# A written issue order for the attention of an encoder layer, and the zeros of its result rows moved into it

## The chip, the cores and the metric

One core of a Trainium2 chip runs the whole program. The metric is device time in microseconds: 1177.47 us is the median of three runs before the change (1177.21 to 1180.05). One more execution was taken with the hardware profiler; all rows here are of it.

## The reference

One layer of a streaming encoder for 1024 tokens of width 1024, in float32:

```
proj = x @ w_in                       -> q, k, v, u (512 columns each)
a    = differential attention          4 heads, each with two 64-wide score maps; a token sees
                                       its own chunk of 64 and all chunks before it:
       p0, p1 = softmax(q_c k_c / 8);  o = (p0 - lam * p1) @ v
       o = o * rsqrt(mean(o^2) + 1e-5) * subln_g * (1 - lam_init)
s    = S5 state space model on u, gelu, then z = z * sigmoid(z @ w_glu + b_glu)
h    = LayerNorm(alpha * x + concat([a, s]) @ w_out)
y    = LayerNorm(alpha * h + MoE(h))   32 experts in 4 groups, two experts per token
```

## The kernel before

The kernel is one straight program for five engines: TensorE (PE), ScalarE (ACT), VectorE (DVE), GpSimd (POOL) and SyncE (SP), which issues most of the transfers. A planner puts each engine's instructions into an order by a simulated time line; an instruction that is traced earlier has priority, but one that is ready sooner may pass it. Where `tc.add_manual_dep(i, earlier, NoSync)` is given, `i` is issued behind `earlier` on that engine, with no wait for its end. In the kernel before only the experts are ordered in this way, by `keep_order` at the end. SBUF is handed out in 25 buffers of 8 KB per partition, taken from a queue (`sl.get`) and given back (`sl.put`); a buffer's next user waits for its last.

In order of time: the projections of u, the state space model in eight units (`ssm_pair`, each followed by a projection of q or v as a filling), the projections of k, the attention, the mixing products with w_out and the first LayerNorm and routing, the experts, the last LayerNorm.

In the state space part `zeros(u)` writes zeros over `moe_dram`, the 2048 rows of results of the experts (8 MB), from one zeroed tile, two transfers of 1 MB behind each of the units 0 to 3. SP issues them, between the transfers of the state space model (`Tm`, line 581) and the loads of w_in (line 190).

The attention is cut into 32 units, a head h and a block i of 128 query rows; n = 128 (i + 1) keys are seen. Units 0 to 15 alternate head 0 with falling i and head 1 with rising i (sizes 1024, 128, 896, 256 and so on); units 16 to 31 take heads 2 and 3 with falling i, 1024 first. For one unit:

- `scores` (lines 792 and 793): two products for each map c and each 512 keys, the query as a high and a low part. For n up to 512 both maps lie in one PSUM pair; above, each map has a pair of its own. VectorE masks 64 rows with a memset (801 or 809) and takes the negative maximum (802 or 810). ScalarE makes the exponential and its row sum (795). Of the PSUM pairs there are two.
- `weigh`: VectorE makes 1/L (817), the factor rho and p0 + rho * p1 (both in the helper at 163); TensorE transposes the blocks (826); ScalarE copies the first four blocks and VectorE the others (827); TensorE adds up the output products (830).
- `normalize` once per four blocks of a head: copy and square on ScalarE (836, 838), a row sum and small products on VectorE (840, and the helpers at 157 and 169), a power on GpSimd (845), one more small product on VectorE, the scaling on GpSimd; `finish`, three units later, transposes and copies with the factor gcol (852, 853).

The loop traces for each u: the scores of unit u + 2 whole, then `weigh` of unit u, then a `finish`, then the fillings at fixed units: `ask` (queries of heads 2 and 3, units 6 and 12), `glu_prepare` (load of w_glu and splits, units 15 and 20), `glu` (12 products of 512 columns each, units 16 to 19 and 21 to 24), `wo_part` (load and split of a quarter of w_out, units 22, 24, 26 and 30). The splits of the fillings lie on ScalarE and GpSimd. In `glu` the gate is made by ScalarE (749) and GpSimd (169), and multiplied into zT by VectorE (helper at 157).

## Time and profile before

| | us |
|---|---|
| median of three runs | 1177.47 |
| the profiled execution, its own time | 1178.13 |
| its span, first to last instruction | 1176.4 |
| TensorE busy in it | 1083.7 (92%) |
| VectorE busy | 970.0 (82%) |
| ScalarE busy | 708.5 (60%) |
| GpSimd busy | 358.0 (30%) |

A row of a timeline has the start and the duration in us, engine, line, operation, written tile and read tiles; in brackets the idle time of the engine before it and what ended that. A line can be that of a small helper (154 subtract, 157 multiply, 160 add, 163 and 169 scalar forms, 173 the high part of a split), so the names of the tiles tell the step. A row of the groups by line has the count, then the busy time in us and the mean duration of one in ns, then idle time ahead. The starts and durations of TensorE's matmuls overlap, since they are pipelined; the step from one start to the next is what one costs.

### The profile page before, as it was taken

To read this page: it belongs to the slowest core of one execution; us is meant where nothing else is said; L and a number is where in the kernel's file an instruction comes from. 1 tells how busy PE (TensorE), PEld (TensorE's weight loads), DVE (VectorE), ACT (ScalarE), POOL (GpSimd) and SP (SyncE) were. 2 spreads that over 40 slices of the span, in tenths; PEclk is the share of its full clock that TensorE was granted. 3 is DMA by queue.
4 is the path that set the end of the run, shared out by engine and by line. 5 is a ranking of instruction groups with operands and counts; after the bars stand their busy time and mean duration, and the time that the engine had idled before them with its cause. 6 is when DMAs were issued, how large, how long until landed. Compare 5 with 4: busy or idle time off the path is not lost.

```text
span 1176.4 us, 15227 instructions
## 1 busy us (share of the span) xinstructions
PE 1083.7 (92%) x5345; PEld 903.9 (77%) x5345; DVE 970.0 (82%) x1434; ACT 708.5 (60%) x956; POOL 358.0 (30%) x296
## 2 busy tenths in 40 slices
PE   6979998897869989995999999999999999999994
PEld 5867887676758878885888888888888888888862
DVE  4898567556878785456899999999999999999976
ACT  3312332426756653212788888888888888888852
POOL 1077464312453454243121221221221211211133
PEclk9989999898999999996999999999999999999997
DMA  8537321201120346446599999999999999999593
GB/s 209 138 97 259 113 59 29 59 19 41 40 64 4 130 160 217 168 171 242 195 343 386 374 380 389 382 393 392 367 393 381 362 384 379 387 392 386 191 261 149
DMA packets 90686, 278.90 MB, mean 237 GB/s; under 512 B 29468, under 2 KB 49964, under 8 KB 66160
## 3 DMA queue, kind: packets, MB, share of 16 engines
q1 hardware_dynamic: 78080, 252.78, 57.6%
q0 software_dynamic: 11520, 24.83, 7.8%
q8 instruction: 43, 0.70, 0.2%
q10 hardware_dynamic: 1008, 0.30, 0.1%
q14 instruction: 35, 0.29, 0.1%
HBM read 254.12 MB, written 34.60 MB: 245 GB/s over the span
## 4 chain that ended last, share of the span: by engine, by line
PE 69%; DVE 12%; DMA 7%; ACT 4%; SPq 3%; issue 3%; POOL 1%; ACTq 0%; DVEq 0%; POOLq 0%
PE g L1251 15%; PE y L1242 15%; PE u L1251 14%; PE mix L1082 7%; PE proj L243 4%; DMA misc<-in_w_in_dram 3%; PE xT L1212 3%; DMA moe_dram<-zero 2%; PE glu L745 2%; PE po L830 2%; DVE ssm L157 1%; SPq L581 1%; PE hT L1224 1%; PE s L792 1%; PE pl L1104 1%
## 5 line engine op out<-in xcount | busy, mean ns | idle before, releaser
L1151 POOL DMA_INDIRECT moe_dram<-yo,idx x30 | 52.1, 1738 | 425.9 <-DVE yo L163 425.9
L243 PE MATMUL proj<-xh,wa 128*128 128x512 f32 x256 | 77.9, 412 | 4.4 <-ACT ssm L678 4.2
L243 PE MATMUL proj<-xh,wb 128*128 128x512 f32 x256 | 74.5, 404 | 1.6 <-ACT ssm L678 1.6
L1082 PE MATMUL mix<-woh,mx 128*128 128x512 f32 x256 | 73.8, 399 | 1.6 <-DVE mx L154 1.6
L1146 POOL DMA_INDIRECT gx<-h_dram,idx x32 | 60.4, 1889 | 22.5 <-DVE WT L160 13.1
L795 ACT ACTIVATE p<-s,nm 128x1024 f32<-128x1024 f32 (+7 forms) x64 | 47.2, 743 | 24.3 <-DVE nm L810 14.9
L243 PEld LDWEIGHTS proj<-xh,wa 128*128 128x128 f32 x256 | 50.2, 199 | 14.9 <-ACT ssm L678 4.5
L243 PEld LDWEIGHTS proj<-xh,wb 128*128 128x128 f32 x256 | 48.6, 194 | 11.5 <-ACT ssm L678 1.8
L1082 PEld LDWEIGHTS mix<-woh,mx 128*128 128x128 f32 x256 | 47.4, 189 | 11.2 <-DVE mx L154 2.1
L792 PE MATMUL s<-kk,qh 128*128 128x512 f32 (+3 forms) x96 | 37.6, 396 | 18.1 <-ACT p L795 15.0
L1258 ACT ACTIVATE yo<-y,WT 128x1024 f32<-128x1024 f32 (+1 forms) x33 | 36.0, 1091 | 24.4 <-PE y L1242 24.4
L1212 PEld LDWEIGHTS xT<-ident,gx 128*128 128x128 f32 x256 | 36.2, 208 | 9.7 <-DMA gx<-h_dram,idx 5.7
L243 PE MATMUL proj<-xl,wa 128*128 128x512 f32 x128 | 43.6, 412 | 0.0
L1212 PE MATMUL xT<-ident,gx 128*128 128x128 f32 x256 | 36.9, 287 | 6.9 <-DMA gx<-h_dram,idx 5.4
L163 DVE SCALAR_TENSOR_TENSOR yo<-gx,first,yo 128x1024 f32<-128x1024 f32 (+1 forms) x33 | 41.3, 1252 | 1.6
L154 DVE TENSOR_TENSOR xe<-xT,xe 128x1024 fp32r<-128x1024 f32 (+1 forms) x33 | 39.1, 1184 | 4.1 <-ACT xe L173 4.1
L830 PE MATMUL po<-vv,half 128*128 128x128 f32 x288 | 41.0, 285 | 1.4 <-ACT half L827 1.3
L1082 PE MATMUL mix<-wol,mx 128*128 128x512 f32 x128 | 42.1, 397 | 0.0
L243 PE MATMUL proj<-xl,wb 128*128 128x512 f32 x128 | 41.0, 397 | 0.0
L173 ACT CAST xe<-xT 128x1024 fp32r<-128x1024 f32 (+1 forms) x33 | 32.3, 978 | 13.4 <-PE xT L1212 13.4
L830 PEld LDWEIGHTS po<-vv,half 128*128 128x128 f32 x288 | 37.4, 198 | 3.5 <-ACT half L827 2.4
L792 PEld LDWEIGHTS s<-kk,qh 128*128 128x128 f32 x96 | 19.3, 201 | 24.7 <-ACT p L795 22.6
(864 smaller groups left out, 3560.1 us busy)
## 6 DMA issues: line engine op xcount, KB each, us to landing
misc<-in_w_in_dram SPq DMA_DIRECT2D x16, 512.0 KB, 3.9
moe_dram<-zero SPq DMA_DIRECT2D x8, 1024.0 KB, 8.5
xr<-in_x_dram SPq DMA_DIRECT2D x8, 512.0 KB, 8.8
wo_raw<-in_w_out_dram SPq DMA_DIRECT2D x4, 1024.0 KB, 5.1
xa<-in_x_dram SPq DMA_DIRECT2D x8, 512.0 KB, 4.4
h_dram<-xa SPq DMA_DIRECT2D x8, 512.0 KB, 3.6
mo<-moe_dram SPq DMA_DIRECT2D x8, 512.0 KB, 8.6
mo<-moe_dram POOLq DMA_DIRECT2D x8, 512.0 KB, 12.7
```

Of the source, the lines that this page charges most:

```text
L154: eng.tensor_tensor(out=out_, in0=a, in1=b, op=ALU.subtract)
L163: return V.scalar_tensor_tensor(out=out_, in0=a, scalar=s, in1=b, op0=op0, op1=op1)
L243: PE.matmul(o[:, hs], wt[kt // 4][:, w_, kt % 4, :], x_[:, hs], start=(kt == 0 and n == 0), stop=(kt == KT - 1 and n == 2))
L792: PE.matmul(s_[:, c0:c0 + w], qd[0][:, c, tk], kk[h][:, c, c0:c0 + w], start=True, stop=False)
L795: S.activation(p_[:, c, 0:n], s_[:, 0:n], AF.Exp, bias=nm[:, c:c + 1], accum_out=L[:, j, c:c + 1])
L830: PE.matmul(po[:, j * P:(j + 1) * P], aT[:, k, :], vv[k // 4][:, k % 4, h * P:(h + 1) * P], start=(k == 0), stop=(k == i))
L1082: PE.matmul(o[-(hs.start > 0)][:, hs], mx[:, m_, kt, :], (woh, wol)[w_][kt // 2][:, kt % 2, hs], start=(kt == 0 and n == 0), stop=(kt == K ...
L1146: return G.indirect_dma_start(out=dst, out_offset=None, in_=h_dram[:, :], in_offset=bass.IndirectOffsetOnAxis(ap=ix, axis=0), bounds_check ...
L1151: G.indirect_dma_start(out=moe_dram[:, :], out_offset=bass.IndirectOffsetOnAxis(ap=ix, axis=0), in_=src, in_offset=None, bounds_check=2 * ...
L1212: PE.transpose(b_[:, kt * P:(kt + 1) * P], rows(g_, kt), ident)
L1242: PE.matmul(y[h_], hid[e][:, x_, kt, :], w_[:, k, HALVES[h_]], start=(kt == 0 and n == 0), stop=(kt == 3 and n == 2))
L1251: PE.matmul(o, xT[e][:, x_, kt, :], w_[:, k, :], start=(kt == 0 and n == 0), stop=(kt == KT - 1 and n == 2))
```

## The change

The attention loop now traces a unit in steps (the functions become generators): weighing of unit u, first map of the scores of u + 2 (both maps for n up to 512), transposes and copies of u, what ends a group of four blocks, second map of u + 2, output products of u. `tie` then orders PE, ACT and DVE each by the order of tracing, from the first unit to the last, the GLU included; the instructions of `ask`, `glu_prepare` and `wo_part` are left out of it. `keep_order` uses the same function. The norm is rewritten: the sum of squares gets L squared times a constant, and the factor of the width goes into gcol, so that no small product waits for GpSimd's power. The GLU's last product goes from VectorE to GpSimd. `zeros` leaves the state space part; a zero tile is taken at unit 13 and four transfers of 2 MB are traced behind units 13, 14, 16 and 17.

```diff
@@ -35,6 +35,7 @@
            mybir.EngineType.SP)
 NORM = 'VAAVAAAV'
 GB = 0
+ZERO = (13, 14, 16, 17)
 ASK, GLU, WO = (6, 12), (15, 16, 1, 20, 21, 1), (22, 24, 26, 30)
 FILLS = [(ASK[0], ("ask", 2)), (ASK[1], ("ask", 3))]
 for half in range(2):
@@ -651,7 +652,6 @@
             if u + 2 == NG // 4:
                 areas[1].close()
             fill(u)
-            zeros(u)
         if c4 % 2 == 1:
             sl.put(UTs.pop(c4 // 2))
         for tq in range(2):
@@ -695,18 +695,6 @@
         sub(t_[64:P, 1, :], o[64:P, :], t_[0:64, 1, :].bitcast(F32))
         kk[h] = t_
 
-
-    zero = sl.get([P, D], F32, "zero")
-    G.memset(zero, 0.0)
-
-    def zeros(u):
-        for j in range(2 * u, 2 * u + 2) if u < ZU else ():
-            SP.dma_start(moe_dram[256 * j:256 * j + 256, :].rearrange("(p a) n -> p a n", p=P),
-                         zero.unsqueeze(1).broadcast_to([P, 2, D]))
-        if u == ZU - 1:
-            sl.put(zero)
-
-    ZU = 4
     fills = [(proj_q, 0), (proj_q, 1), (proj_q, 2), (proj_q, 3), (proj_v, 0), (proj_v, 1), (proj_v, 2), (proj_v, 3)]
     made[0] = ssm_prepare(0)
     for c4 in range(4):
@@ -749,7 +737,7 @@
         S.activation(sg, o, AF.Tanh, bias=bg[:, ct:ct + 1], scale=0.5)
         ts(sg, sg, 0.5, ALU.mult, 0.5, ALU.add, eng=G)
         z_ = zT[ct // 2][:, ct % 2, hs]
-        mul(z_, z_, sg)
+        mul(z_, z_, sg, G)
         if ct == 3:
             sl.put(zh, zl)
             if half == 1:
@@ -760,11 +748,23 @@
     G.memset(mhalf, -0.5)
     gcol = cp.tile([P, 1], F32, name="gcol")
     PQ.dma_start(gcol, I["subln_g"][0].rearrange("(p o) -> p o", o=1), allow_slow_non_contiguous=True)
-    ts(gcol, gcol, 1.0 - LAM_INIT, ALU.mult)
+    ts(gcol, gcol, (1.0 - LAM_INIT) * math.sqrt(P), ALU.mult)
     aoT = {}
 
     def sm(name, n, bufs=4):
         return cp.tile([P, n], F32, tag=name, name=name, bufs=bufs)
+
+    def tie(traced, engines):
+
+        prev = {}
+        for i in traced:
+            if i.engine not in engines:
+                continue
+            if i.engine in prev:
+                tc.add_manual_dep(i, prev[i.engine].name,
+                                  mybir.DependencyInfo(mybir.DependencyClass.NoSync, mybir.DependencyReason.DATA),
+                                  reason="keep_order")
+            prev[i.engine] = i
 
     def queries(h):
 
@@ -802,14 +802,14 @@
             V.tensor_reduce(out=nm, in_=s2[:, :, 0:n], axis=AX.X, op=ALU.max, negate=True)
             for c in range(2):
                 weights(s2[:, c, :], c)
-        else:
-            for c in range(2):
-                s_ = bank2(f"s{h}_{i}_{c}")
-                products(s_, c)
-                V.memset(s_[0:64, n - 64:n], -1e30)
-                V.tensor_reduce(out=nm[:, c:c + 1], in_=s_[:, 0:n], axis=AX.X, op=ALU.max, negate=True)
-                weights(s_, c)
-        return p_
+            yield p_
+        for c in range(2 if n > 512 else 0):
+            s_ = bank2(f"s{h}_{i}_{c}")
+            products(s_, c)
+            V.memset(s_[0:64, n - 64:n], -1e30)
+            V.tensor_reduce(out=nm[:, c:c + 1], in_=s_[:, 0:n], axis=AX.X, op=ALU.max, negate=True)
+            weights(s_, c)
+            yield p_
 
     def weigh(h, i, p_, L, RL, j, po):
 
@@ -818,6 +818,7 @@
         rho = sm("rho", 1)
         stt(rho, L[:, j, 0:1], nlam, RL[:, j, 1:2], ALU.mult, ALU.mult)
         stt(p_[:, 0, 0:n], p_[:, 1, 0:n], rho, p_[:, 0, 0:n], ALU.mult, ALU.add)
+        yield
         aT = half.get("aT", [8, P], bufs=2)
         for k0 in range(0, i + 1, 4):
             k1 = min(k0 + 4, i + 1)
@@ -826,25 +827,28 @@
                 PE.transpose(b_[:, (k - k0) * P:(k - k0 + 1) * P], p_[:, 0, k * P:(k + 1) * P], ident)
             (V.tensor_copy if k0 else S.copy)(aT[:, k0:k1, :], b_[:, 0:(k1 - k0) * P].rearrange("p (k q) -> p k q", q=P))
         sl.put(p_)
+        yield
         for k in range(i + 1):
             PE.matmul(po[:, j * P:(j + 1) * P], aT[:, k, :], vv[k // 4][:, k % 4, h * P:(h + 1) * P],
                       start=(k == 0), stop=(k == i))
-
-    def normalize(h, g, po, RL):
+        yield
+
+    def normalize(h, g, po, L):
 
         sq = half.get("sq", [2, 512], bufs=2)
         S.copy(sq[:, 1, :], po)
         o4 = sq[:, 1, :].rearrange("p (j e) -> p j e", j=4)
         S.activation(sq[:, 0, :], sq[:, 1, :], AF.Square)
-        ss = sm("ss", 4, 2)
-        V.tensor_reduce(out=ss, in_=sq[:, 0, :].rearrange("p (j e) -> p j e", j=4), axis=AX.X, op=ALU.add)
-        r0 = RL[:, :, 0]
-        mul(ss, ss, r0)
-        mul(ss, ss, r0)
-        ts(ss, ss, 1.0 / P, ALU.mult, EPS, ALU.add)
-        G.tensor_tensor(out=ss, in0=ss, in1=mhalf, op=ALU.pow)
-        mul(ss, ss, r0)
-        mul(o4, o4, ss.unsqueeze(2).broadcast_to([P, 4, P]), G)
+
+        ss, l2 = sm("ss", 4, 2), sm("l2", 4, 2)
+        mul(l2, L[:, :, 0], L[:, :, 0])
+        ts(l2, l2, EPS * P, ALU.mult)
+
+        def scale():
+            V.tensor_reduce(out=ss, in_=sq[:, 0, :].rearrange("p (j e) -> p j e", j=4), axis=AX.X, op=ALU.add)
+            add(ss, ss, l2)
+            G.tensor_tensor(out=ss, in0=ss, in1=mhalf, op=ALU.pow)
+            mul(o4, o4, ss.unsqueeze(2).broadcast_to([P, 4, P]), G)
 
         def finish():
             b_ = bank(f"ot{h}_{g}")
@@ -852,7 +856,7 @@
                 PE.transpose(b_[:, j * P:(j + 1) * P], sq[:, 1, j * P:(j + 1) * P], ident)
             S.mul(aoT[g][:, h, :], b_, gcol)
 
-        return finish
+        return scale, finish
 
     proj_k(0)
     qd = {0: queries(0)}
@@ -876,10 +880,16 @@
         if (h, i // 4) not in grp:
             grp[h, i // 4] = (sm("L", 8, 4).rearrange("p (j c) -> p j c", c=2),
                               sm("RL", 8, 4).rearrange("p (j c) -> p j c", c=2), bank(f"po{h}_{i}", 1))
-        live[u] = scores(h, i, qd[h], grp[h, i // 4][0], i % 4)
+        live[u] = steps = scores(h, i, qd[h], grp[h, i // 4][0], i % 4)
+        p_ = next(steps)
+        yield
+        for _ in steps:
+            pass
+        live[u] = p_
         starts[h] = starts.get(h, 0) + 1
         if starts[h] == NT:
             sl.put(*qd.pop(h), kk.pop(h))
+        yield
 
     woh, wol = [], []
 
@@ -901,23 +911,53 @@
         fills.setdefault(u, []).append(what)
     LEAD, LATE = 2, 3
     late = {}
+    first_pin = len(nc.cur_bb.bb.instructions)
     for u in range(LEAD):
-        start(u)
+        for _ in start(u):
+            pass
+    done, apart = {}, set()
     for u, (h, i) in enumerate(units):
-        if u + LEAD < len(units):
-            start(u + LEAD)
         L_, RL_, po_ = grp[h, i // 4]
-        weigh(h, i, live.pop(u), L_, RL_, i % 4, po_)
+        old = weigh(h, i, live.pop(u), L_, RL_, i % 4, po_)
+        new = start(u + LEAD) if u + LEAD < len(units) else iter(())
+        next(old)
+        next(new, None)
+        next(old)
+        scales = [normalize(*done.pop(x)) for x in list(done)]
+        next(new, None)
+        for sc, fin in scales:
+            sc()
+            late[u + LATE - 1] = fin
+        next(old)
         if u in late:
             late.pop(u)()
         ends[h, i // 4] = ends.get((h, i // 4), 0) + 1
         if ends[h, i // 4] == 4:
-            late[u + LATE] = normalize(h, i // 4, po_, RL_)
+            done[u] = h, i // 4, po_, L_
+        if u == ZERO[0]:
+
+            zero = sl.get([P, D], F32, "zero")
+            G.memset(zero, 0.0)
+        if u in ZERO:
+            j = 512 * ZERO.index(u)
+            SP.dma_start(moe_dram[j:j + 512, :].rearrange("(p a) n -> p a n", p=P),
+                         zero.unsqueeze(1).broadcast_to([P, 4, D]))
+        if u == ZERO[3] + 2:
+            sl.put(zero)
         if u in fills:
             for f_, *a_ in fills[u]:
+                at = len(nc.cur_bb.bb.instructions)
                 {"ask": ask, "pre": glu_prepare, "glu": glu, "wo": wo_part}[f_](*a_)
+                if f_ != "glu":
+                    apart.update(range(at, len(nc.cur_bb.bb.instructions)))
+    for x in list(done):
+        sc, fin = normalize(*done.pop(x))
+        sc()
+        late[len(units) + x] = fin
     for f_ in late.values():
         f_()
+    tie([i for k, i in enumerate(nc.cur_bb.bb.instructions) if k >= first_pin and k not in apart],
+        (mybir.EngineType.PE, mybir.EngineType.Activation, mybir.EngineType.DVE))
     sl.put(*vv.values())
     half.close()
 
@@ -1339,16 +1379,8 @@
 
     def keep_order():
 
-        traced, prev = nc.cur_bb.bb.instructions, {}
-        at = next(k for k, i in enumerate(traced) if i is pins[0])
-        for i in traced[at:]:
-            if i.engine not in ORDERED:
-                continue
-            if i.engine in prev:
-                tc.add_manual_dep(i, prev[i.engine].name,
-                                  mybir.DependencyInfo(mybir.DependencyClass.NoSync, mybir.DependencyReason.DATA),
-                                  reason="keep_order")
-            prev[i.engine] = i
+        traced = nc.cur_bb.bb.instructions
+        tie(traced[next(k for k, i in enumerate(traced) if i is pins[0]):], ORDERED)
 
     def refill():
         while st_["load"] < min(len(order), st_["split"] + deep(st_["load"])[1]):
```

## Rows read from the trace of the kernel before

**Rows 1.** Windows by stage: start:end, length, each engine's busy us, clock, DMA share, GB/s.

```profile
87.00:272.70 185.70, 170.44 (x863) 142.41 (x863) 120.27 (x160) 63.61 (x97) 91.03 (x70) 0.95 0.29 89
282.90:355.00 72.10, 54.99 (x343) 47.26 (x344) 61.17 (x128) 47.61 (x102) 29.55 (x22) 0.95 0.17 45
355.00:405.00 50.00, 48.82 (x304) 43.06 (x302) 40.26 (x85) 29.94 (x60) 16.34 (x13) 1.00 0.13 43
405.00:426.40 21.40, 16.28 (x91) 13.45 (x90) 18.54 (x36) 16.58 (x44) 14.95 (x12) 0.92 0.64 201
...
560.00:1176.40 616.40, 598.47 (x2771) 494.31 (x2769) 581.02 (x567) 481.71 (x532) 130.74 (x93) 0.99 0.92 347
```

**Rows 2.** Chain of waits in order of time, 70 to 300: start, us, what.

```profile
113.30 11.25 DMA moe_dram<-zero
```

**Rows 3.** Waits of TensorE, 90 to 130: total us, times, longest.

```profile
PE py L627 <- DVE ssm L154: 2.7, 2, 1.9
```

**Rows 4.** Timeline, 357.9 to 361.9, one map of a unit with n = 896.

```profile
357.94 0.39 PE L792 MATMUL s<-kk,qh 128*128 128x512 f32 x1
...
358.99 0.11 DVE L809 MEMSET s<- 64x64 f32 x1 [0.78 <-PE s L793]
359.13 1.09 DVE L810 TENSOR_REDUCE nm<-s 128x1 f32<-128x896 f32 x1
...
360.32 1.01 ACT L795 ACTIVATE p<-s,nm 128x896 f32<-128x896 f32 x1 [1.43 <-DVE nm L810]
```

**Rows 5.** Timeline, 353.5 to 355.2: a copy and the output products after it.

```profile
353.56 0.59 ACT L827 COPY half<-at 128x512 f32<-128x512 f32 x1 [0.47 <-PE at L826]
...
354.20 1.16 PE L830 MATMUL po<-vv,half 128*128 128x128 f32 x8 [0.24 <-ACT half L827]
```

**Rows 6.** Groups by line and shape of VectorE and of ScalarE, 262 to 428.

```profile
L163 DVE SCALAR_TENSOR_TENSOR rho<-L,nlam,RL 128x1 f32<-128x1 f32 x31 | 15.9, 513 | 0.6
L810 DVE TENSOR_REDUCE nm<-s 128x1 f32<-128x1024 f32 x8 | 9.7, 1217 | 0.1
...
L157 DVE TENSOR_TENSOR zT<-zT,wg_raw 128x512 f32<-128x512 f32 x8 | 7.0, 872 | 0.6 <-POOL wg_raw L169 0.5
L810 DVE TENSOR_REDUCE nm<-s 128x1 f32<-128x640 f32 x8 | 6.5, 816 | 0.1
...
L802 DVE TENSOR_REDUCE nm<-s 128x2 f32<-128x1024 f32 x4 | 4.9, 1220 | 0.1
...
L802 DVE TENSOR_REDUCE nm<-s 128x2 f32<-128x256 f32 x4 | 1.7, 423 | 0.1
...
L795 ACT ACTIVATE p<-s,nm 128x1024 f32<-128x1024 f32 x8 | 8.9, 1113 | 4.4 <-DVE nm L810 4.4
...
L795 ACT ACTIVATE p<-s,nm 128x128 f32<-128x128 f32 x6 | 2.2, 373 | 0.0
```

**Rows 7.** Chain of waits in order of time, 268 to 430.

```profile
355.36 2.75 PE glu L745 x12
...
358.90 0.89 PE po L830 x8
...
426.45 3.48 PE mix L1082 x14
```

**Rows 8.** Timeline of SP's queue, 225 to 430.

```profile
421.40 0.38 SPq L891 DMA_DIRECT2D wo_raw<-in_w_out_dram  x1
```

**Rows 9.** Instructions on tile rho, 262 to 432: min, median, max ns.

```profile
L163 DVE SCALAR_TENSOR_TENSOR rho<-L,nlam,RL x32: 148/219/2624, 283.1 to 430.4; 128x1 f32<-128x1 f32 x32
```

**Rows 10.** Timeline, 294 to 299: GpSimd's splits and VectorE.

```profile
294.06 4.81 POOL L154 TENSOR_TENSOR ql<-qr,qh 64x1024 fp32r<-64x1024 f32 x2
...
296.66 2.23 DVE L163 SCALAR_TENSOR_TENSOR rho<-L,nlam,RL 128x1 f32<-128x1 f32 x1
```

**Rows 11.** Instructions on tile ss, 262 to 432: min, median, max ns.

```profile
L157 DVE TENSOR_TENSOR ss<-ss,RL x18: 136/148/2277, 312.1 to 417.3; 128x4 f32<-128x4 f32 x18
...
L157 POOL TENSOR_TENSOR half<-half,ss x6: 1040/1042/1053, 316.5 to 417.5; 128x512 f32<-128x512 f32 x6
```

## The prediction

> **What bounds the kernel now.** The windows by stage come first [rows 1]. From 560 us on TensorE is busy 598.47 of 616.40 us: the experts run as one unbroken string of products, so a delay or a gain ahead of them is carried to the end one for one. The reader is to compare three stretches of the attention. From 355 to 405 TensorE is busy 48.82 of 50.00 us: nothing on another engine is late there, because the planner puts the scores of a later unit, the GLU products and the output products in any order that is ready. From 282.9 to 355 it is busy 54.99 of 72.10, from 405 to 426.4 it is 16.28 of 21.40. So the attention can win at most 17.1 + 5.1 = 22.2 us of idle TensorE, and it can lose far more if the freedom of the middle stretch goes. In the stage ahead, from 87 to 272.7, TensorE is idle 15.3 us of 185.7.
>
> Second, the chain of waits: it runs through a zero transfer twice, the longer time 11.25 us [rows 2]. But TensorE itself waited only 2.7 us in that stretch [rows 3]: the zeros are late links of a chain that runs beside busy products.
>
> Third, one unit of the attention, followed through the engines in the timeline [rows 4, 5]. Scores start on TensorE at 357.94, the mask memset on VectorE at 358.99, the maximum at 359.13 for 1.09 us, the exponential on ScalarE at 360.32. A copy of four transposed blocks on ScalarE starts at 353.56, and the output products that need it at 354.20, 0.64 us later.
>
> **The change, part by part.** *The tie.* Inside the loop the engines now keep the written order. For iteration u it is, on TensorE: scores of unit u+2 (its first half c=0 where n is over 512, both halves otherwise), transposes of u, scores c=1, output products of u, a head's transposes, GLU. On ScalarE: exponential c=0 of u+2, copy of the transposes of u, exponential c=1. On VectorE: the weighing of u, mask and maximum c=0 of u+2, copy of blocks over four, mask and maximum c=1. Read as waits, this is one closed string per iteration: the copy of u stands behind the exponential of u+2, which needs the maximum of u+2, which needs the scores of u+2, which on TensorE stand behind the output products of u-1, which need the copy of u-1. So nothing of iteration u+1 on this string can begin before iteration u's has ended. Transposes, c=1 and weighing lie beside it. Its sum over 30 units (units 0 and 1 are scored ahead of the loop):
> - Scores to mask: 1.05 us for n = 896 [rows 4], of which 0.80 are its 1792 columns at GLU's rate (12 products of 512 columns in 2.75 us, [rows 7]) and 0.25 the handover. Scaled by columns: 1.17, 1.05, 0.94, 0.82 for the large units, and, both halves together, 1.17, 0.94, 0.71, 0.48 for the small ones; four heads make 29.1, less units 0 and 1 (1.17 + 0.48) = 27.5.
> - Mask to maximum 0.14 x 30 = 4.2; maximum to exponential 0.10 x 30 = 3.0 [rows 4].
> - Maxima: large units, one of two maps, 1217 to 816 ns over four sizes in even steps, times four heads 16.3; small ones, both maps in one, 1220 to 423 ns, 13.1 [rows 6]; less 1.22 and 0.42 = 27.8.
> - Exponentials: 1113 ns for n = 1024 and 373 for n = 128 [rows 6], 106 ns per 128 keys between; large units, one map, 15.3; small ones, both maps, 17.0; less 1.11 and 0.75 = 30.4.
> - Copy to output products: 20 units with four or more blocks at 0.64 [rows 5], the 12 smaller ones at 0.53, 0.43 and 0.31 (scaled by blocks) = 17.9.
> - Output products: 0.89 us for four blocks [rows 7], 144 blocks = 32.0.
>
> Sum 142.8. GLU stands on TensorE between the output products of u and the scores of u+3, so it no longer fills a gap but lengthens the string: 8 x 2.75 [rows 7] = 22.0. Seven heads' transposes (four blocks, half of 0.89) add 3.1. Together 167.9 us, from 282.9 to 450.8.
>
> What follows the attention waits less than that: the last quarter of w_out is issued at 421.40 [rows 8], 5.0 us before the mixing products run on at 426.45 [rows 7]. It needs a buffer that unit 27 gives back after its transposes. Behind these stand the output products of 27 and the short units 28 to 31: two of 2.8 us, two of 0.6, and 1.2 = 8.0 us, which can run between mixing products. So mixing begins at 450.8 - 8.0 + 5.0 = 447.8 instead of 426.4: +21.4. The gap that it costs shows as TensorE waiting for the copy: about 168 less some 115 of its own work (120.1 in the three stretches, less the first mixing products), 50 us in all.
>
> *VectorE against GpSimd.* The sum above is free of stretches. In the trace VectorE's tiny rho step takes 513 ns in the mean and 219 in the median, 31 of them [rows 6, 9]: 9.1 us. The row at 296.66 shows one: 2.23 us, ending as GpSimd's two splits (294.06, 4.81 us) end [rows 10]. These splits stay as they are and are not tied. If slack of VectorE in the longer iterations hides all of them, 0; if all fall on the string again, 9.1 and the 1.5 of the GLU product (872 ns against 684) = 10.6. I take 6, past the middle, since the weighing that is hit stands ahead of the maximum in VectorE's order. The GLU product moved to GpSimd takes 8 x 872 ns = 7.0 us off VectorE [rows 6], and the norm's three small products of 148 ns per group (18 in the stretch) become one product and one scaling that wait for nothing [rows 11]: both were on VectorE, which is not on the string outside its maxima, so I cost them at nothing; their cover is the wait of VectorE for scores.
>
> GpSimd's own product of that shape takes 1042 ns [rows 11]. The Trainium skill (SBUF — State Buffer, Who interferes with whom) says that a VectorE instruction with two SBUF inputs is blocked for the whole of a GpSimd instruction that reads SBUF. By that rule the moved products could give back 8 x 1.04 = 8.3 us of block for the 7.0 they save; by the row at 296.66 only an instruction that meets one pays. The sum above uses neither.
>
> *The zeros.* Eight transfers of 1 MB and a memset leave the stage 87 to 272.7. Bounds: 0, if TensorE stays full; 15.3, all of its idle time there [rows 1]. I take 3, next to the 2.7 us that it waited while they ran [rows 3]. In their new place four transfers of 2 MB go through SP, where only the loads of w_glu (unit 15) and w_out wait; 1 MB landed after up to 11.25 us [rows 2], and two pieces are written ahead of w_glu. Bounds 0 to 22.5 us (twice that) for a late w_glu; I take 0, since from its split to the first GLU at unit 16 the string is slow as well.
>
> Sum: +21.4 + 6 - 3 = +24.4 on the profiled execution's 1178.13 (span 1176.4 and 1.7 around it), which lies 0.7 above the median of 1177.47: **1202 us**.
>
> **The rivals.** *The written order is the better one* (faster). It would be so if a planner that goes by its own costs lost more to late scores than the string does. For it: the 17.1 us of idle TensorE from 282.9 to 355, with VectorE busy 61.17 of 72.10 there, and the work taken from VectorE. Against it: TensorE was full for 50 us because scores did not wait for the copy of the unit before, and that freedom goes. It decides at the mean step of an iteration: the loop had 143.5 us for 30, 4.8 with GLU; under that it wins. With half of 22.2 closed and 3 for the zeros: 1163; with all, 1152.
>
> *The tie changes little, the zeros pay.* If the order of the planner is near the written one, only the zeros count: -3 to -15.3, about 1168. Against it: the dense stretch 355 to 405 cannot be had from the written order.
>
> *GLU waits for its weights.* With two zero transfers ahead of w_glu, units 16 on are late by 11.25 to 22.5 us, and with TensorE tied nothing passes the GLU products. Added to the forecast: 1213 to 1225, say 1219. Against it: units 13 to 15 last three iterations of 4.8 us in the mean (142.8 / 30), in which the zeros drain.
>
> **How the numbers follow.** What this measurement tells from no change is about 0.3%, 3.5 us. Forecast 0.62, its own range 1184 (zeros 15.3, no stretch: +6) to 1226 (no overlap at the tail, +8; all stretches, +4.6; a w_glu late by one landing, +11.25); GLU late 0.10; written order better 0.21; zeros alone 0.07. Slower: 0.61 + 0.10 = 0.71. Faster: 0.20 + 0.05 = 0.25. Within: 0.01 + 0.01 + 0.02 = 0.04. The range 1160 to 1226 leaves out the better half of the first rival's gain, some 0.08, and as much above it.
>
> **What would show it.** Right: TensorE's waits for ScalarE's copy (line 827) grow from about 1 us to some 50; ScalarE waits for the maxima and VectorE for scores, iteration after iteration; no stretch of 50 us with TensorE full; the last w_out load some 20 us later; the stage to 272.7 only a little shorter. Wrong: TensorE busy over 90% in the tied loop, or scores of u+2 starting before the output products of u-1; then the first rival holds.

## The result, and the profile after

The changed kernel takes 1237.67 us (median of 4 runs, 1237.23 to 1237.84), the one before 1178.42 us beside it (4 runs, 1177.21 to 1180.05): the ratio is 1.051, 95% interval 1.049 to 1.053. Slower, as forecast, but by 59 us and not by 24, and 12 us over the end of the range. The two profiled executions have spans of 1235.9 and 1176.4 us, 59.5 apart; the account below is made on these. Loop means the attention loop, and its iteration u is the one that weighs unit u.

Windows of the changed kernel by stage (start:end, length, each engine's busy us, TensorE's granted clock, DMA share, GB/s). They answer to [rows 1].

```profile
87.00:266.00 179.00, 168.88 (x866) 142.00 (x866) 117.56 (x161) 63.66 (x97) 89.89 (x70) 0.96 0.18 45
276.20:440.00 163.80, 113.64 (x617) 97.16 (x618) 98.65 (x188) 76.31 (x156) 54.53 (x42) 0.86 0.24 84
440.00:477.50 37.50, 22.99 (x107) 19.60 (x106) 16.45 (x35) 17.36 (x39) 22.44 (x16) 0.73 0.38 117
584.20:616.20 32.00, 14.25 (x89) 12.87 (x89) 20.62 (x79) 7.01 (x12) 9.43 (x9) 0.67 0.54 192
616.20:1235.90 619.70, 601.33 (x2779) 496.66 (x2777) 582.88 (x568) 484.08 (x535) 130.39 (x93) 0.99 0.91 346
```

Three things can be seen. The stage ahead of the attention ends at 266.0 instead of 272.7. The loop, from its third unit to the first mixing products, takes 201 us and no engine is full in it: TensorE is busy 136.6 of 201.3 us, every other engine less. There is no stretch like [rows 1]' 355 to 405, where TensorE was full. And TensorE's granted clock in the loop is 0.86 and then 0.73, where before it was 0.95, 1.00 and 0.92. From the experts on nothing differs.

TensorE's waits, 255 to 500 (total us, times, longest), and four rows of the chain of waits at the end of the loop:

```profile
PE po L832 <- ACT half L828: 59.8, 26, 6.0
PE s L792 <- ACT p L795: 5.5, 2, 3.3
PE at L827 <- DVE p L164: 3.6, 4, 1.7
```

```profile
467.28 4.78 DMA wo_raw<-in_w_out_dram
...
473.11 1.04 ACT woh L174
474.15 0.71 ACT p L795 x4
...
477.58 2.48 PE mix L1122 x7
```

The wait named as the sign of the chain is there: the output products wait for ScalarE's copy 26 times, 59.8 us in all (before: 1.3 us). Mixing runs on at 477.58 instead of 426.45 [rows 7], +51.1 us; the forecast had +24.4 in all. After that another 8.4 us come: 2.9 up to the first products of the routing tables (529.87 before, 583.95 now), 5.3 from there to the experts' first products, 0.2 in the rest.

**The chain, measured link by link.** One iteration at nearly the forecast length, and one that is far over it. Timeline, changed kernel, 307 to 312 (start, us, engine, line, operation; in brackets what ended the idle time before it):

```profile
307.00 0.17 DVE L801 MEMSET s<- 64x128 f32 x1 [1.34 <-PE s L793]
307.20 1.22 DVE L802 TENSOR_REDUCE nm<-s 128x2 f32<-128x1024 f32 x1
...
308.52 0.69 ACT L795 ACTIVATE p<-s,nm 128x512 f32<-128x512 f32 x1 [2.86 <-DVE RL L817]
...
309.20 0.68 ACT L795 ACTIVATE p<-s,nm 128x512 f32<-128x512 f32 x1
...
309.86 0.48 ACT L828 COPY half<-at 128x384 f32<-128x384 f32 x1
310.39 0.94 PE L832 MATMUL po<-vv,half 128*128 128x128 f32 x6 [3.23 <-ACT half L828]
311.08 0.47 PE L792 MATMUL s<-kk,qh 128*128 128x512 f32 x1
```

Mask, maximum, two exponentials, copy, output products, next scores: each begins as the one before it ends, and TensorE stood 3.23 us for it. The same kernel from 350 to 360:

```profile
352.11 1.22 DVE L810 TENSOR_REDUCE nm<-s 128x1 f32<-128x1024 f32 x1
...
354.10 1.99 ACT L174 CAST wgh<-wg_raw 128x1024 fp32r<-128x1024 f32 x2 [3.92 <-DMA wg_raw<-in_w_glu_dram]
...
355.23 4.64 POOL L155 TENSOR_TENSOR wgl<-wg_raw,wgh 128x1024 fp32r<-128x1024 f32 x2 [5.82 <-DVE nm L810]
355.28 2.30 DVE L164 SCALAR_TENSOR_TENSOR rho<-L,nlam,RL 128x1 f32<-128x1 f32 x1
355.99 1.99 ACT L174 CAST zh<-zT 128x1024 fp32r<-128x1024 f32 x2
357.62 2.40 DVE L164 SCALAR_TENSOR_TENSOR p<-p,rho 128x128 f32<-128x128 f32 x1
357.89 1.11 ACT L795 ACTIVATE p<-s,nm 128x1024 f32<-128x1024 f32 x1
...
358.99 0.57 ACT L828 COPY half<-at 128x512 f32<-128x512 f32 x1
```

The maximum is ready at 353.33, its exponential begins at 357.89. Between them ScalarE did four casts of the GLU's operands. They are not in the written order, so ScalarE had them where the planner put them, ahead of this exponential; ScalarE stood 3.92 us for the transfer that the first needs. An instruction that is not tied can so stand in the chain all the same.

Laid out so for iterations 1 to 27, from the start of the copy of the unit before to the start of this unit's copy, the links sum to this (us). Each link runs from start to start, along the first half of the scores (the one whose exponential the copy stands behind), and the output products are those that are read. The first column is the prediction's terms for the same links, with the GLU in the second; "filled" is `e6_fill_waits`, "casts" `e7_casts_gpsimd`, "both" `e11_fill_and_casts` and "copies" `e13_tied_extra`, all below.

```
link                                forecast  changed  filled  casts  both   copies
copy -> output products                 15.9     15.7    17.1   16.0   19.4    15.8
output products -> next scores          52.0     66.1    57.3   64.3   55.8    73.9
scores -> mask                          25.4     36.3    33.4   41.5   36.6    39.3
mask -> maximum                          3.8      4.8     4.8    4.8    4.8     4.8
maximum -> exponential                  28.5     37.8    43.3   30.0   31.6    33.4
exponential -> copy                     28.0     27.2    27.2   27.2   27.2    46.8
sum                                    153.6    188.0   183.1  183.6  175.3   213.9
```

The chain is the forecast one, and three of its six links are within 1 us of the forecast. The other three hold the 34.4 us. 17.3 are where TensorE is the slower one: 11.4 in output products and GLU (after 2.7 for heads' transposes, which the prediction had as a term of its own), and 5.9 from scores to mask where VectorE waited for the scores. 9.3 are where casts stand ahead of an exponential (iterations 1, 13, 18, 24 and 26: 1.3, 4.5, 1.4, 1.0, 1.1). And 4.9 are five iterations in which VectorE came late to the mask. The slower TensorE is seen in the rows of iteration 7: ten output products, then the scores at 318.22 and 318.79:

```profile
316.06 2.50 PE L832 MATMUL po<-vv,half 128*128 128x128 f32 x10 [2.52 <-ACT half L828]
318.22 0.77 PE L792 MATMUL s<-kk,qh 128*128 128x512 f32 x1
318.79 0.63 PE L793 MATMUL s<-kk,ql 128*128 128x512 f32 x1
```

From the first product of 512 columns to the next are 0.57 us, and 0.43 from there to the one behind; where TensorE is kept busy (an experiment below) the same three start 0.32 and 0.23 us apart. The granted clock from 316 to 319 is 0.50. So this is the lower of its two levels, 1.2 against 2.4 GHz, after a wait of 2.52 us and others like it before. Not all of the 17.3 is the clock: in the column "both", where the granted clock is 0.98 and 1.00, 3.5 of it stay. The Trainium skill (TensorE: Matmul & The Clock Gate, Part 1: The HAM clock gate) says that the throttled clock is the default and that activity releases it; the granted 0.86 and 0.73 of this loop, 32% of which TensorE was idle, agree.

### The profile page after: what moved, and what is told of

The parts are those of the page before. It is cut to its first block, busy times and chain, and to the rows that moved or that the text cites. A ratio compares the mean times of both kernels' runs of the same rounds, so it can differ in the third digit from the quotient of the medians.

```text
span 1235.9 us, 15263 instructions
## 1 busy us (share of the span) xinstructions
PE 1099.6 (89%) x5345; PEld 917.1 (74%) x5345; DVE 963.1 (78%) x1418; ACT 708.7 (57%) x956; POOL 368.5 (30%) x304
## 4 chain that ended last, share of the span: by engine, by line
PE 58%; DVE 3%; ACT 3%; issue 3%; DMA 2%; POOL 2%; SPq 0%; ACTq 0%; DVEq 0%; POOLq 0%
PE y L1282 13%; PE u L1291 13%; PE g L1291 13%; PE mix L1122 7%; PE xT L1252 2%; PE po L832 2%; PE glu L733 2%; DMA mo<-moe_dram 2%; PE hT L1264 1%; PE pl L1144 1%; ACT p L795 1%; DVE mo L164 1%; PE hT L1140 1%; DVE nm L810 1%; ACT half L828 0%
## 5 line engine op out<-in xcount | busy, mean ns | idle before, releaser
L832 PE MATMUL po<-vv,half 128*128 128x128 f32 x288 | 49.8, 330 | 60.0 <-ACT half L828 59.8
L832 PEld LDWEIGHTS po<-vv,half 128*128 128x128 f32 x288 | 43.2, 231 | 68.1 <-ACT half L828 67.9
L1298 ACT ACTIVATE yo<-y,WT 128x1024 f32<-128x1024 f32 (+1 forms) x33 | 36.0, 1092 | 24.4 <-PE y L1282 24.4
L792 PE MATMUL s<-kk,qh 128*128 128x512 f32 (+3 forms) x96 | 41.6, 434 | 5.5 <-ACT p L795 5.5
L164 DVE SCALAR_TENSOR_TENSOR p<-p,rho 128x1024 f32<-128x1024 f32 (+7 forms) x32 | 37.6, 1175 | 1.5 <-DVE rho L164 0.3
```

Source lines behind the costliest of these rows:

```text
L164: return V.scalar_tensor_tensor(out=out_, in0=a, scalar=s, in1=b, op0=op0, op1=op1)
L792: PE.matmul(s_[:, c0:c0 + w], qd[0][:, c, tk], kk[h][:, c, c0:c0 + w], start=True, stop=False)
L832: PE.matmul(po[:, j * P:(j + 1) * P], aT[:, k, :], vv[k // 4][:, k % 4, h * P:(h + 1) * P], start=(k == 0), stop=(k == i))
```

## The experiments

**Which part of the change costs it.** The theory is the closed chain of the written order. Rivals: the zeros in the loop hold up the GLU's weights; GpSimd's new product; TensorE's clock.

`e1_untied`, the written order alone taken out:

```
-    tie([i for k, i in enumerate(...) if k >= first_pin and k not in apart],
-        (mybir.EngineType.PE, mybir.EngineType.Activation, mybir.EngineType.DVE))
```

> The written order alone is taken out (the call that ties the three engines); the zeros stay in their four pieces, the normalisation and the GLU product stay as changed. Theory (the string of waits that the order makes: scores, maximum, exponential, copy, output products): TensorE's wait for ScalarE's copy falls from 59.8 us to under 8, the loop from its third unit to the mixing falls from 201 us to 145-155, and the time is 1165-1180 us. Rival A (zeros behind the GLU's weights, and GpSimd's GLU product, stretch VectorE and delay the GLU): most of the loss stays, 1210 us or more. Rival B (TensorE's low clock is its own cause): the clock stays under 0.9 in the loop and the time over 1200 us.

Measured 1187.1 us (1180.6 to 1190.3), ratio to before 1.006 (1.003 to 1.010). TensorE's wait for the copy falls from 59.8 to 0.2 us. So some 50 of the 59 us are the order's; the time is 7 us over what was expected, which the last group of experiments takes up.

`e4_zeros_back`, the order kept, the zeros again in eight pieces in the state-space stage:

```
             fill(u)
+            zeros(u)                   # as before: two pieces behind each of four units
...
-        if u in ZERO:
-            ...
```

> The changed kernel with the zeros back in their place of before (eight pieces in the state-space stage). My theory: the attention begins 6.7 us later, and nothing in the loop hangs on the zeros but the GLU's weights (their landing up to 5 us): 1238-1245 us. Rival A (the zeros in the loop delay the GLU and through the tied order everything): 1210-1228 us.

Measured 1242.5 us (1.056, 1.053 to 1.059): 4.8 slower than the changed kernel. The zeros' new place helps, with the attention beginning at 266.0 and not at 271.0. And the cast of the GLU's weights still waits for their transfer, with no zeros near it:

```profile
358.11 1.99 ACT L174 CAST wgh<-wg_raw 128x1024 fp32r<-128x1024 f32 x2 [3.98 <-DMA wg_raw<-in_w_glu_dram]
```

3.98 us against 3.92: the prediction's third rival falls. The wait is the transfer's own length, at the head of a queue that now holds the chain.

`e9_zeros_alone`, the kernel before with nothing but the zeros moved (the same lines the other way, on the kernel before):

> The kernel before with the zeros alone moved behind units 13, 14, 16 and 17, nothing else changed. The state-space stage ends 6.7 us earlier, as in the changed kernel, and no order is written. If nothing takes it back: 1168-1174 us. Rival A (the zeros' queue delays the GLU's weights, which land behind nothing else, and the loop loses what the stage gained): 1176-1188 us.

Measured 1175.7 us (10 runs), ratio 0.997 (0.995 to 0.999): the one version that beats both kernels, by about what can be told apart. Its scores begin at 265.0, 7.7 us earlier, and mixing ends 3.2 us earlier; between the expectation and the rival. Its chain of waits now runs through the transfer of the GLU's weights, 6.63 us from 325.43, where the kernel before had one of 5.62 from 332.19. That this is where the gain went was not tested apart.

**Is it the closed chain?** It needs the orders of TensorE, ScalarE and VectorE at once. Two kernels free one engine each, one moves the output products.

`e2_scalar_free`:

```
-        (mybir.EngineType.PE, mybir.EngineType.Activation, mybir.EngineType.DVE))
+        (mybir.EngineType.PE, mybir.EngineType.DVE))
```

> The written order holds TensorE and VectorE as in the changed kernel, ScalarE is free of it. Theory (string): the copy that the output products wait for no longer stands behind the next unit's exponential by order, so TensorE's wait for the copy falls from 59.8 us to under 20 and the time is 1190-1212 us; what is left is TensorE's and VectorE's own written order. Rival C (the order of TensorE itself, its transposes waiting for VectorE's weighted sums, is the whole loss): 1228-1238 us. Rival D (unpinned casts ahead on ScalarE): they still stand there, 1225-1240 us.

Measured 1192.5 us (1.012, 1.009 to 1.015).

`e18_tensor_free`:

```
-        (mybir.EngineType.PE, mybir.EngineType.Activation, mybir.EngineType.DVE))
+        (mybir.EngineType.Activation, mybir.EngineType.DVE))
```

> The written order holds ScalarE and VectorE, TensorE is free of it. Theory (the chain closes only if all three keep the order: it passes from the output products of a unit to the scores of the unit three on by TensorE's order alone): cut as with ScalarE free, 1188-1205 us, and TensorE's wait for the copy falls under 20 us. Rival (ScalarE's order alone, copy behind exponential, is what costs): 1225-1240 us.

Measured 1196.8 us (1.016, 1.014 to 1.018).

`e3_products_later`, all three engines tied:

```
         next(old)                      # transposes and copy of unit u
+        if held is not None:
+            next(held)                 # output products of unit u-1
+            tail(u - 1)
...
-        next(old)
+        held = old
```

> All three engines tied, but the output products of a unit are written one iteration later, behind the transposes of the unit after it, so that the copy has a whole iteration. Theory (string): the closed chain is cut; TensorE's wait for the copy falls from 59.8 us to under 8, and the chain that is left (second half's scores, its maximum 1.2 us, weighted sum 1.4-2.4 us, transposes) gives 4.3-5 us an iteration for the long units: time 1175-1202 us. Rival B (the clock) and rival D (casts on ScalarE that stand ahead of exponentials): 1215-1235 us, since both stay.

Measured 1197.3 us (1.017, 1.015 to 1.020). TensorE's waits, 255 to 500, first with ScalarE free, then with the products later:

```profile
PE s L792 <- ACT p L795: 12.2, 5, 5.0
PE po L832 <- ACT half L828: 10.6, 15, 1.6
PE at L827 <- DVE p L164: 10.1, 8, 2.4
```

```profile
PE at L827 <- DVE p L164: 27.2, 12, 5.4
PE s L792 <- ACT p L795: 10.0, 4, 4.3
PE at L827 <- DVE s L809: 6.9, 6, 2.0
```

Each of the three cuts gives back 40 to 45 us, whichever link it opens. So neither ScalarE's nor TensorE's order by itself is the cost, but the ring that closes through both is; VectorE was not freed alone. In the third kernel a smaller chain takes its place: transposes wait for VectorE's weighing, which stands behind a maximum. `e15_weighed_early` writes the weighing of unit u+1 between the two maxima of unit u+2, in an iteration of its own ahead:

```
+        nxt = weighed(u + 1)           # before the second half of unit u+2
```

> All three engines tied, output products one iteration later (1197.3 us), and here the weighing of unit u+1 written one iteration earlier, between the two maxima of unit u+2, so that the transposes find it done (TensorE waited 27.2 us for it there). Theory (a written order loses by its closed chains alone, and TensorE's 120 us of work then bounds the loop): 1178-1192 us. Rival (each tied order loses some 15 us, whatever it is): 1195-1205 us.

Measured 1191.7 us (1.013, 1.010 to 1.016), the upper end of what the theory gave; the wait for the weighed sums is 2.5 us there. `e16_early_casts` adds the casts on GpSimd (the edit of `e7_casts_gpsimd` below):

> The same, with the casts of the GLU's and the projection's operands on GpSimd. Theory (what stays in the tied loop are ScalarE's casts that wait for a transfer at the head of its queue): 5-10 us under the kernel without this edit, 1170-1185 us, about the time of before. Rival (GpSimd's longer way holds the mixing up): 1-8 us over it.

Measured 1189.1 us (1.008, 1.006 to 1.010): lower by 2.6, not by 5 to 10. So a written order needn't cost 50 us; none tried here reached the planner's time.

**One link made longer.** `e13_tied_extra` and `e14_untied_extra` add one copy of the same size on ScalarE ahead of each unit's copy:

```
+            if not k0:
+                S.copy(aT[:, k0:k1, :], vv[0][:, 0:k1, 0:P])
             (V.tensor_copy if k0 else S.copy)(aT[:, k0:k1, :], ...)
```

> The changed kernel with one more copy on ScalarE in each unit, written just ahead of the copy of the transposed blocks, of its size (20 of 0.58, 4 each of 0.48, 0.37 and 0.26 us: 16.0 us in all), into the same buffer, which the real copy then overwrites. ScalarE is busy only 76 of 164 us in the loop. Theory (one closed chain in which each copy stands between an exponential and the output products): each added copy lengthens the chain by its whole length, +13 to +16 us, 1250-1254 us. Rival (ScalarE has slack in the iterations and the loop's length lies with TensorE and VectorE): +0 to +5 us, 1238-1243 us.

Measured 1264.3 us (1.074, 1.072 to 1.077): +26.6, more than the copies' whole length.

> The same 32 added copies in the kernel without the written order (1187.1 us). Theory: without the order the copies lie beside other work, +0 to +6 us, 1187-1193 us. Rival (ScalarE's own work bounds the loop with or without the order): +13 to +16 us, 1200-1203 us.

Measured 1177.6 us (0.999, 0.998 to 1.001): 9.5 us faster than the same kernel without the copies. In the tied kernel each copy is paid for in full, and 10 us more; in the untied one it costs nothing; that the planner, which goes by its own costs, placed the rest better around them is my reading of the 9.5 us, and is not shown. The added copies took 17.0 us in the trace (the expectation took 16.0, the length of the real ones), so the rest is 9.6. The last column of the table shows it. Exponential to copy grew by 19.6, of which some 15.8 are the copies (608 ns for the largest) and 3.8 two pairs of casts that stood here; maximum to exponential, where one of these pairs had stood, fell by 4.4. The output products with the GLU grew by 7.8 and scores to mask by 3.0, with nothing added to them. Windows of the kernel with copies, 276.2 to 477.5:

```profile
276.20:440.00 163.80, 109.59 (x553) 94.90 (x553) 88.32 (x170) 81.29 (x160) 49.69 (x37) 0.79 0.22 77
440.00:477.50 37.50, 25.27 (x109) 21.21 (x107) 13.11 (x28) 14.28 (x28) 12.21 (x12) 0.82 0.18 59
```

The clock fell to 0.79 where it had been 0.86. (From 440 on the two kernels are in different iterations, and 0.82 can't be held against 0.73.)

**What the sum had left out.** `e6_fill_waits` keeps TensorE busy in its waits: six products more a unit, just ahead of the output products, which overwrite them.

```
+        for k in range(WARM):          # WARM = 6
+            PE.matmul(po[:, j * P:(j + 1) * P], ident, vv[0][:, 0, h * P:(h + 1) * P], start=True, stop=True)
```

> The changed kernel with six products more in each of the 32 units, written between the transposes and the output products, on data long there and overwritten by the output products (nothing reads them): they stand in TensorE's wait for ScalarE's copy, 1.4-2 us a unit. Theory B (the clock that falls to 0.72-0.86 in the waits is a large part of what my sum missed): the granted clock of 276 to 440 rises from 0.86 over 0.93 and the time falls by 8 to 20 us, to 1218-1230 us. Theory S (the chain's time lies on ScalarE and VectorE, the clock is only a sign of it): within 5 us of 1238 us, or slower by up to 20 us where the products outlast the wait.

Measured 1236.0 us (1.047, 1.043 to 1.051), 1.7 under the changed kernel: by the time alone, theory S. The windows and the table say more.

```profile
276.20:440.00 163.80, 132.72 (x910) 119.43 (x911) 95.08 (x191) 77.58 (x158) 54.88 (x42) 0.96 0.25 85
440.00:477.50 37.50, 26.81 (x189) 24.34 (x189) 19.03 (x47) 21.56 (x54) 22.26 (x16) 1.00 0.42 135
```

The products of iteration 7 in this kernel, to be held against those at 318.22 above:

```profile
316.03 0.48 PE L793 MATMUL s<-kk,qh 128*128 128x512 f32 x1
316.35 0.40 PE L794 MATMUL s<-kk,ql 128*128 128x512 f32 x1
316.58 0.22 PE L793 MATMUL s<-kk,qh 128*128 128x128 f32 x1
```

The clock is 0.96 and 1.00. Output products to scores fell by some 9 us and scores to mask by 2.9; copy to output products, where the fillings can stand in the way, grew by 1.4. But maximum to exponential grew by 5.5: the loop came earlier to the cast that stands for the GLU's weights and stood there 2.5 us longer, and the rest lies almost wholly at two other pairs of casts (1.8 and 1.2). `e7_casts_gpsimd` takes that away:

```
-        S.copy(hi, raw)
+        (cast.tensor_copy if cast else S.copy)(hi, raw)    # cast = GpSimd for the GLU and w_out
```

> The changed kernel with the 14 casts of the GLU's and the output projection's operands (14.0 us of ScalarE, and 9.4 us that ScalarE stood waiting ahead of them) moved to GpSimd. Theory D (casts outside the written order stand on ScalarE ahead of the copies and exponentials that the chain hangs on, and each adds its time to the chain): the time falls by 12 to 25 us, to 1213-1226 us. Rival (they lie in ScalarE's idle time, and GpSimd is later with the weights): 1233-1250 us.

Measured 1229.0 us (1.042, 1.038 to 1.047): −8.6, between the two expectations. Maximum to exponential fell by 7.8, to 30.0 against a forecast of 28.5. But scores to mask grew by 5.2, 3.8 of them in iteration 15, where VectorE's weighing now lies beside GpSimd's splits, which come later behind the casts:

```profile
362.76 3.33 DVE L164 SCALAR_TENSOR_TENSOR p<-p,rho 128x1024 f32<-128x1024 f32 x1
```

In the changed kernel a weighing of this size takes 1.28 us (at 374.22). In all, the 27 iterations gave 4.4 us; the other half of the 8.6 came outside them.

`e11_fill_and_casts` has the last two edits together:

> The two single edits together: the six filling products a unit (TensorE's clock rose to 0.95-1.00, 1236.0 us) and the casts on GpSimd (1229.0 us). The first gained 8 us in the products of the chain and lost as much where a cast that waits for the GLU's weights stood on ScalarE, which the second takes away. If clock and casts are two terms of what my sum missed: 1217-1224 us. If the fillings cost what the clock gives: 1227-1233 us.

Measured 1218.2 us (1.035, 1.033 to 1.037): −19.5, as two terms that hide behind one another should give. Last, `e17_extra_and_fill`, the same filling on the kernel with the added copies:

> The changed kernel with the 32 added copies on ScalarE (alone 1264.3 us, +26.6, of which the copies themselves are 16.0) and with the six filling products a unit (alone 1236.0 us). Theory (the 10.6 us over the copies' own length are TensorE's products at half clock, since longer waits lower its clock): the fillings take that back, 1248-1254 us. Rival (the copies cost their place in the queue more than their length, whatever the clock): 1259-1265 us.

Measured 1255.2 us (1.065, 1.063 to 1.067), with the clock at 0.93 and not 0.79. Against the filled kernel the copies now cost 19.2 us, 2.2 over their own length and not 9.6. The time lies 1 us over the theory's range and 4 us under the rival's.

**The rest of the change**, without the written order. `e10_untied_glu_vector` puts the GLU's product back on VectorE, `e12_old_norm` also the normalisation's old arithmetic:

```
-        mul(z_, z_, sg, G)
+        mul(z_, z_, sg)
...                                     # and in the second kernel
-            add(ss, ss, l2)
+            mul(ss, ss, r0)
+            mul(ss, ss, r0)
+            ts(ss, ss, 1.0 / P, ALU.mult, EPS, ALU.add)
             G.tensor_tensor(out=ss, in0=ss, in1=mhalf, op=ALU.pow)
+            mul(ss, ss, r0)
```

> The changed kernel without the written order (1187.1 us), and with the GLU's product back on VectorE. That kernel still lost 15 us of the loop after the 6.7 us that the zeros gave. If GpSimd's product (8 of 1.27 us, each ahead of the splits that the mixing waits for) is the cause: 1172-1180 us. If it is the order of tracing that the new loop gives the planner, or the normalisation: 1184-1190 us.

> No written order, GLU's product on VectorE, zeros in the loop (1184.5 us), and here also the normalisation's arithmetic as before (three products of 148 ns and the scaling), but still called one iteration later as the changed loop has it. If the new arithmetic costs what is left between that kernel and the zeros alone (1175.7 us): 1174-1178 us. If the loop's new order of tracing does: 1183-1187 us.

Measured 1184.5 us (1.005, 1.002 to 1.007) and 1179.3 us (1.002, 0.999 to 1.004). The single runs of the first spread from 1179.0 to 1189.2, and the 32 idle copies moved the untied kernel by as much. The 8.8 us between the first of the two and the zeros alone are therefore not divided among GLU, normalisation and the new order of tracing; that stays open.

## Why the prediction was wrong

- **The direction and the mechanism were right.** The three written orders make one closed string (the ring above); TensorE waits for the copy (forecast some 50 us, 59.8 found); no stretch with TensorE full is left. The first rival put its turning point at 4.8 us an iteration: the loop needs 201.3 / 30 = 6.7.
- **The step that failed is the sum of the string, 142.8 us (with the GLU 164.8): its terms were of the right links at the wrong speed, and one link was missing.** Scores, output products and GLU were taken from rows of a TensorE that had been busy (0.23 us for 512 columns, 0.89 for four blocks), and then the string was found to leave TensorE waiting for a third of the time. In that string they run at the lower clock for long stretches: 17.3 us where TensorE is late, of which 13.8 are gone in the kernel "both", at a clock of 0.98 and 1.00.
- **The casts were not in the string at all.** The prediction listed ScalarE's order from the written loop alone, and left out what stays outside the tie but goes through the same queue: 9.3 us in the 27 iterations. Moving 14 of the casts away took 7.8 off that link; that the time fell by 8.6 is near it by luck, since 5.2 came back at the mask and as much was won elsewhere.
- **VectorE** came to 4.9 us where 6 were taken, and that they are near is luck. The 6 stood for steps stretched beside GpSimd's splits, and only 1.6 of the 4.9 are such (the 219-ns step that takes 2.35 us at 293.00, iteration 3). 3.2 are the norm, which the prediction put at nothing. In iterations 8, 9 and 16 its row sum waits for ScalarE's square, and in the written order the weighing and the mask stand behind it:

```profile
323.43 0.69 DVE L848 TENSOR_REDUCE ss<-half 128x4 f32<-128x512 f32 x1 [0.53 <-ACT half L841]
...
324.68 0.75 DVE L164 SCALAR_TENSOR_TENSOR p<-p,rho 128x512 f32<-128x512 f32 x1
325.45 0.17 DVE L801 MEMSET s<- 64x128 f32 x1
```

The scores under this mask had ended at 324.16. The stretched steps themselves are there, as in [rows 10]: the row at 355.28 above takes 2.30 us for 219 ns. The Trainium skill (SBUF — State Buffer, Who interferes with whom) says that a VectorE instruction with two SBUF inputs contends with a GpSimd instruction that reads SBUF; the trace agrees, since from 276 to 478 the nine steps on rho or the weighed sum that take 1.7 us or more all lie beside GpSimd's splits. But eight of the nine are not on the chain.
- **The zeros** gave more than the 3 us taken: the attention begins 6.7 us earlier. The time shows 4.8 of them under the written order and 3.0 without it. The GLU's weights were not made late by them.
- **After the string** the forecast had nothing. The short units at the end and the start of mixing took 4.8 us more than their term; 1.8 of it is unit 30's exponentials (474.15 above), which stood behind casts of w_out that had waited for its load. And 8.4 came behind that, 5.3 of them ahead of the experts, where TensorE waits for VectorE's ranks (6.2 us once) that it had waited 3.3 for before. No run takes these apart.

So, at the start of mixing: 24.4 forecast, +17.3 TensorE, +9.3 casts, −1.1 VectorE, −3.7 zeros, +4.8 tail, +0.1 in the other links = 51.1; and +8.4 behind it = 59.5.

The range failed for the same reason: its upper end added only lateness that single rows showed, and held the string's own terms fixed.

## What to carry to other kernels

Read a written order as queues: follow one unit through all engines, and look for a ring in which an instruction stands behind another unit's work; to move the output products by one iteration was worth 40 us here. When a sum gives a chain that leaves TensorE waiting, look for rows of its products at the lower clock, and put into the chain every instruction that shares a queue with it, tied or not, above all one that waits for a transfer. And compare a planner's kernel with more than one placement of it: idle copies added to one made it 9.5 us faster here.

## What the runs showed that was not expected

- Work added to a waiting chain costs more than its length: 17.0 us of added ScalarE copies cost 26.6 us (1264.3 against 1237.7), and 19.2 where TensorE was kept busy with products that nobody reads (1255.2 against 1236.0), with its clock at 0.79 and at 0.93.
- Six idle products a unit lower the time of the output products they stand ahead of: the 248 of them from 276 to 440 take 325 ns in the mean without, 292 with. Groups of TensorE, 276 to 440, the changed kernel and the filled one:

```profile
L832 PE MATMUL po<-vv,half 128*128 128x128 f32 x248 | 41.3, 325 | 45.5 <-ACT half L828 45.3
```

```profile
L835 PE MATMUL po<-vv,half 128*128 128x128 f32 x248 | 35.3, 292 | 23.8 <-ACT half L829 23.5
```

- A cast by itself is hardly dearer on GpSimd: 1084 ns for 128 x 1024 in the kernel with the casts there, against 1043 on ScalarE in the changed kernel (eight each, w_out's; GpSimd's spans are rough). GpSimd's group, 276 to 478:

```profile
L174 POOL CAST woh<-wo_raw 128x1024 fp32r<-128x1024 f32 x8 | 8.4, 1084 | 3.6 <-DMA wo_raw<-in_w_out_dram 3.6
```
